# Hybrid attention and gMLP backbone on one core: query projection computed transposed, attention values by column halves of the array, and a new step order ahead of the first output projection

## The chip, the cores and the metric

The program runs on one core of a Trainium2 chip. Five engines with instruction streams of their own work side by side: TensorE (PE in the profile; its weight loads are listed apart as PEld), VectorE (DVE), ScalarE (ACT), GpSimd (POOL) and SyncE (SP), which here only issues transfers. An engine takes its instructions in the order in which they stand. They wait for each other through semaphores. Matmul results land in PSUM (eight banks of 128 partitions by 512 fp32 numbers); everything else stands in SBUF.

The metric is the device time of one execution in microseconds; several runs of one kernel are told by their median. The profile shows one execution. Its span runs from the first to the last instruction of the engines.

## The reference, cut to what matters

A two-layer backbone works on 512 latent tokens and 256 context tokens of width 1024, all in fp32. Layer 0 uses windowed attention with grouped heads; layer 1 uses a gated MLP over chunks. A dense SwiGLU network follows each. Only the latent stream is returned. What the change touches is the attention of layer 0:

```
h_l = modulate(rmsnorm(x, norm_g[0, 0]), sh_ml, sc_ml)          # (512, 1024)
h_c = modulate(rmsnorm(ctx_s, norm_g[0, 0]), sh_mc, sc_mc)      # (256, 1024)
q, k, v = split(h_l @ w_qkv, [1024, 1280])                      # 16 query heads, 4 key/value heads, width 64
q = apply_rope(q, cos, sin) * 64 ** -0.5
k = apply_rope(k, cos, sin)
k_c, v_c = split(h_ctx @ w_qkv[:, 1024:], 2)
# per block of 128 queries: keys of the block before, its own and the next one, and all 256 context keys
p = softmax([q k_band^T + mask, q k_c^T, sink])                 # four query heads share a key/value head
o = p_band v_band + p_ctx v_c
y = o @ w_o
```

`apply_rope` splits a head in two halves of 32 columns: `[x1*c - x2*s, x2*c + x1*s]`.

## The kernel before

**Numbers.** The kernel keeps fp32 accuracy with fp32r matmuls, which are cheaper than fp32 ones: a matrix is split in a high part (rounded to fp32r by ACT, `high`) and a low part (what is left, by DVE or POOL, `low`), and a product is three matmuls, high by high, high by low and low by high (`mm3`). Transposes and the attention values use full fp32; the records show each fp32 matmul as two.

**Stages ahead of the first output projection.** First the token tiles come in (four of x, numbered 0 to 3, two of the context, 4 and 5), are normalised, transposed on PE (`turn_in`) and modulated. The modulation vectors come from eight transfers of 1 MB (`ada0_fetch`) and small matmuls (`ada0_rows`, one 32-column strip of the array each, then `ada0_cols` and `ada0_done`). Then keys and values are projected (`kv`, for eight slices k of the model width and six token tiles), each product streaming 512 columns. Keys are rotated, duplicated along the partitions, transposed (`k_turn`) and split into `khi` and `klo`.

**Queries before.** Query heads come in eight groups p: a key/value head g = p // 2 with its four heads, for one half (256) of the tokens. `q_first` (groups 0 and 1) and `q_step` (the others) project with the tokens as the stationary operand (`q_project`, line 273 to 275): the result has tokens on the partitions and 256 columns. ACT copies it out (`q_rows`), POOL and DVE multiply by the cosine and sine tables (`rotate`), DVE adds (`q_add`), ACT and DVE scale and split into high and low, side by side (`q_split`), PE transposes the four heads for each of two token tiles (`q_turn`, line 759), and ACT copies the transposed tile out (line 760). The partitions of that tile hold 64 high and 64 low parts, and one matmul against the duplicated `khi`, one against `klo`, gives the scores (`score`, line 905).

**Blocks.** Sixteen blocks m (query tile t = m % 4, key/value head g = m // 4) run through `score`, `bound` (mask, row maximum; DVE), `exp` (ACT), `sink`, `total`, `normalise` (POOL), `turn` (PE transposes of the probabilities, line 938), `turned` (copies to SBUF by ACT and DVE), `value` and the store. Blocks at both ends have four key tiles (nb = 4), the others five. `value` (line 958) multiplies a key tile's 128 by 64 values with the probabilities of the four heads, 512 columns; even key tiles use the left 64 columns of the array and odd ones the right, so the two halves of `o_ps` are partial sums over key tiles. ACT copies the right half out (`rows_out`, line 963), and DVE adds both halves into `oT` (`store`, line 969, twice a block).

**Work in between.** The first half of the output projection (`wo_part`, after the first two heads' blocks) and the adaLN rows m2, m4 and m3 (`Ada`: eight multiply-adds on DVE, a fold by a POOL transfer, a mirror by an SP transfer, a stack, and a matmul) run between the blocks. All of this is issued in an order written out by hand, the table `ORDER`: each step's name has a place there, and steps are issued in that order on all engines at once. A step missing in it follows by its planned time.

**Transfers.** SP issues nearly all of them, one after the other; an issue whose buffer is not free, or whose data is not there, holds up those behind it. Weight units (`wfetch`) and adaLN chunks share two buffers of 1 MB (`raw`).

Of the kernel before, what the change touches and what calls it, by code (L numbers as in the profile page):

```python
# [41 lines left out]
x_fetch_4 x_fetch_5 square_in_4 x_fetch_1 warm_0 warm_1 dma dma#2 wfetch_0_0 x_fetch_2 x_fetch_0 x_fetch_3 m2start  # L42
rstd_in_4 square_in_5 square_in_1 warm_2 warm_3 rstd_in_5 rstd_in_1 norm_in_4_0 norm_in_5_1 norm_in_1_0 turn_in_4_0
square_in_2 norm_in_1_1 turn_in_1_0 warm_4 square_in_0 turn_in_5_1 norm_in_5_0 rstd_in_2 norm_in_2_0 turn_in_5_0
ada0_fetch_0 turned_in_4_0 square_in_3 rstd_in_0 turn_in_1_1 turned_in_5_0 turned_in_1_0 turn_in_2_0 ada0_rows_0
rstd_in_3 norm_in_2_1 ada0_rows_out_0 norm_in_3_1 <lambda> norm_in_3_0 ada0_cols_0 turn_in_3_1 turned_in_5_1
ada0_fetch_1 norm_in_0_0 turn_in_0_0 norm_in_0_1 ada0_done_0 turn_in_2_1 ada0_fetch_2 whigh_0_0 wfetch_0_1 ada0_rows_1
modulate0_ctx_0 turn_in_0_1 turn_in_3_0 turned_in_3_1 modulated_ctx_0 ada0_rows_out_1 ada0_fetch_3 turned_in_1_1
wlow_0_0 dma#5 turned_in_2_0 ada0_fetch_4 ada0_cols_1 turned_in_0_0 kv_0_4 turned_in_3_0 ada0_rows_2 modulate0_0
wfetch_1 modulated_high_0 ada0_done_1 turned_in_2_1 ada0_rows_out_2 modulated_low_0 ada0_cols_2 kv_0_2 dma#4 kv_0_3  # L50
modulated_high_1 modulate0_ctx_1 kv_0_5 ada0_done_2 modulate0_1 modulated_ctx_1 whigh_0_1 ada0_fetch_6 ada0_rows_3
norm_in_4_1 turn_in_4_1 ada0_rows_out_3 modulated_low_1 modulate0_ctx_2 kv_1_2 kv_1_4 kv_1_5 turned_in_0_1
turned_in_4_1 modulated_high_2 ada0_cols_3 modulate0_2 modulated_ctx_2 kv_0_0 modulated_low_2 ada0_fetch_5 whigh_1_0
wlow_0_1 ada0_rows_4 wfetch_2 wlow_1_0 whigh_1_1 ada0_done_3 kv_1_3 kv_2_4 ada0_fetch_7 kv_2_5 modulate0_3
ada0_rows_out_4 modulated_high_3 kv_1_0 kv_0_1 kv_2_3 kv_1_1 modulate0_ctx_3 modulated_ctx_3 ada0_cols_4 ada0_done_4
# [148 lines left out]
def backbone_kernel(ctx: ExitStack, tc: tile.TileContext, a, out):  # L204
# [465 lines left out]
    def q_first(p, t, k):  # L670
        if t == 0 and k == 0:
            q_ps[p] = bankA("q0")
        q_project(q_ps[p][:, t * 256:(t + 1) * 256], Q0, 2 * p + t, k)
# [152 lines left out]
    def q_turns(p, i, bank):  # L826
        if i == 0:
            qTs[p] = new_qT()
# [1227 lines left out]
```

## Time and profile before

| What | Value |
|---|---|
| Median of 3 runs | 1110.29 us (1109.47 to 1112.27) |
| Span of the profiled execution | 1108.2 us, granted TensorE clock 0.999 |
| What the median has beside that span | 2.1 us |
| PE busy | 1088.3 us, 98% of the span |
| DVE, ACT, POOL busy | 85%, 55%, 23% of the span |
| First matmul of keys and values | starts at 21.43 us |
| Last matmuls of keys and values | start at 69.22 to 69.69 us |
| First score matmul | starts at 81.08 us |
| First matmul of the output projection proper (`y`, line 281) | starts at 239.24 us |

The profile is of one execution on its one core. In rows of the order of time, a matmul's length is modelled and runs into the next one's; what a matmul costs PE is the distance from its start to the start of the next. Rows of the groups give the mean length of one instruction of a kind and how long its engine had stood idle before it.

### The profile page before, as it was taken

The page shows a single profiled execution, that of the slowest core. Times are in us where ns is not written, and L with a number is a line of the kernel's source. Part 1 is how long each engine was busy: PE and PEld are TensorE (multiplying, and loading weights), DVE is VectorE, ACT ScalarE, POOL GpSimd, SP SyncE. Part 2 cuts the span into 40 slices and gives each one's busy share as a digit, 9 for nine tenths or more (in the row PEclk, how much of TensorE's full clock was granted, in tenths as well). Part 3 has the DMA queues.
Part 4 walks back from the last instruction along what each step waited for, and adds up shares of the span by engine and source line. Part 5 has one row for each costly group of instructions (what it writes and reads, how often), then busy time and mean ns, then how long its engine had stood idle before and what let it go on. Part 6 is the DMA issues. An engine that isn't in the chain of part 4 may idle for free.

```text
span 1108.2 us, 17883 instructions
## 1 busy us (share of the span) xinstructions
PE 1088.3 (98%) x6974; PEld 954.9 (86%) x6974; DVE 943.8 (85%) x1418; ACT 612.6 (55%) x1060; POOL 255.9 (23%) x276
## 2 busy tenths in 40 slices
PE   7999999999999999999999999999999999999997
PEld 4788877768799999998888788887999999998876
DVE  5788988958999999987988778878988888879985
ACT  6457767756555545545665534337555545546652
POOL 2517575624600000001321411006400000002300
PEclk9999999999999999999999999999999999999999
DMA  9652333243245655449964286652233343369821
GB/s 366 266 182 86 136 96 115 77 135 113 109 143 172 224 159 185 171 141 330 225 122 128 68 323 241 205 194 77 70 133 124 132 152 126 126 222 319 158 40 76
DMA packets 48857, 179.15 MB, mean 162 GB/s; under 512 B 4859, under 2 KB 9211, under 8 KB 37637
## 3 DMA queue, kind: packets, MB, share of 16 engines
q1 hardware_dynamic: 41220, 163.34, 42.3%
q0 software_dynamic: 7552, 14.68, 7.9%
q8 instruction: 54, 0.88, 0.3%
q14 instruction: 31, 0.25, 0.1%
HBM read 171.71 MB, written 2.10 MB: 157 GB/s over the span
## 4 chain that ended last, share of the span: by engine, by line
PE 64%; DVE 6%; POOL 2%; issue 2%; ACT 1%; DMA 1%; POOLq 0%; DVEq 0%; SPq 0%; ACTq 0%
PE f L1449 35%; PE y L1633 13%; PE y L1660 4%; PE v L281 4%; PE y L281 2%; PE u L1869 1%; PE u L1867 1%; PE u L1868 1%; POOL tmp L1166 1%; DVE w_lo L224 1%; DVE tmp L1170 1%; DVE x L1154 1%; PE mix L1882 1%; DMA w_raw<-in_w 1%; DVE a_sum L1378 1%
## 5 line engine op out<-in xcount | busy, mean ns | idle before, releaser
L1449 PE MATMUL f<-H,w_hi 128*128 128x256 f32 x960 | 178.6, 284 | 1.1 <-DVE fc L1460 0.5
L1449 PEld LDWEIGHTS f<-H,w_hi 128*128 128x128 f32 x960 | 149.7, 192 | 2.3 <-DVE fc L1460 1.4
L1449 PE MATMUL f<-H,w_lo 128*128 128x256 f32 x480 | 135.8, 283 | 0.0
L1633 PE MATMUL y<-w_hi,s 128*128 128x512 f32 x448 | 120.1, 389 | 0.0
L1449 PE MATMUL f<-S,w_hi 128*128 128x256 f32 x640 | 118.6, 283 | 0.0
L217 ACT CAST w_hi<-w_raw 128x1024 fp32r<-128x1024 f32 x90 | 94.5, 1053 | 39.9 <-PE y L1633 8.9
L217 ACT CAST w_hi<-T 128x1024 fp32r<-128x1024 f32 x80 | 83.7, 1047 | 52.4 <-PE f L1449 33.7
L1456 ACT COPY fc<-f 128x256 f32<-128x256 f32 x120 | 44.6, 372 | 105.8 <-PE f L1449 102.7
L224 DVE TENSOR_TENSOR w_lo<-w_raw,w_hi 128x1024 fp32r<-128x1024 f32 (+1 forms) x81 | 96.3, 1193 | 6.7 <-ACT w_hi L217 6.7
L1449 PEld LDWEIGHTS f<-S,w_hi 128*128 128x128 f32 x640 | 99.9, 192 | 0.0
L1633 PEld LDWEIGHTS y<-w_hi,s 128*128 128x128 f32 x448 | 84.1, 188 | 17.5
L224 DVE TENSOR_TENSOR w_lo<-T,w_hi 128x1024 fp32r<-128x1024 f32 x80 | 97.3, 1216 | 0.0
L1449 PEld LDWEIGHTS f<-H,w_lo 128*128 128x128 f32 x480 | 92.1, 192 | 0.0
L1449 PE MATMUL f<-S,w_lo 128*128 128x256 f32 x320 | 90.7, 284 | 0.5 <-DVE w_lo L224 0.5
L1621 POOL DMA_DIRECT2D t<-in_w x48 | 42.2, 929 | 186.5 <-PE y L1660 88.4
L383 DVE SCALAR_TENSOR_TENSOR acc<-ada_k,sc,acc 128x1024 f32<-128x1024 f32 x56 | 71.6, 1278 | 10.3 <-DMA ada_k<-in_ada 8.4
L397 POOL DMA_DIRECT2D acc<-acc x8 | 6.9, 866 | 314.2 <-DVE acc L383 310.4
L1633 PE MATMUL y<-w_lo,s 128*128 128x512 f32 x224 | 69.1, 390 | 0.6 <-DVE w_lo L224 0.6
L1449 PE MATMUL f<-H,x 128*128 128x256 f32 x480 | 64.3, 283 | 0.0
L932 POOL TENSOR_SCALAR p<-p,st 128x512 f32<-128x512 f32 (+1 forms) x64 | 53.4, 849 | 44.4 <-DVE st L928 11.7
L281 PE MATMUL y<-w_hi,st 128*128 128x512 f32 x224 | 62.3, 391 | 0.0
L1449 PEld LDWEIGHTS f<-S,w_lo 128*128 128x128 f32 x320 | 61.4, 192 | 0.9 <-DVE w_lo L224 0.9
(255 smaller groups left out, 2851.6 us busy)
## 6 DMA issues: line engine op xcount, KB each, us to landing
w_raw<-in_w SPq DMA_DIRECT2D x67, 1024.0 KB, 5.0
ada_k<-in_ada SPq DMA_DIRECT2D x56, 512.0 KB, 5.2
ada_raw<-in_ada SPq DMA_DIRECT2D x12, 1024.0 KB, 4.8
w<-in_w SPq DMA_DIRECT2D x12, 1024.0 KB
t<-in_w POOLq DMA_DIRECT2D x48, 256.0 KB, 6.1
ada<-in_ada SPq DMA_DIRECT2D x8, 1024.0 KB, 11.2
t<-in_w SPq DMA_DIRECT2D x8, 1024.0 KB, 9.2
w_raw<-in_w SPq DMA_DIRECT2D x10, 512.0 KB, 5.6
```

The lines of the kernel that those rows point to most:

```text
L217: nc.scalar.copy(out=hi, in_=src)
L224: (eng or nc.vector).tensor_tensor(out=v(lo), in0=v(src), in1=v(hi).bitcast(F32), op=ALU.subtract)
L281: nc.tensor.matmul(dst, l, w[:, n * 512:(n + 1) * 512], start=first and i == 0, stop=last and i == 2)
L383: nc.vector.scalar_tensor_tensor(out=self.acc, in0=self.raws.pop(k), scalar=sc[:, k:k + 1], in1=self.acc, op0=ALU.mult, op1=ALU.add)
L932: nc.gpsimd.tensor_scalar(out=p, in0=p, scalar1=self.st[:, 12 + j:13 + j], scalar2=1.0, op0=ALU.mult, op1=ALU.mult)
L1154: nc.vector.scalar_tensor_tensor(out=xt, in0=self.tmp[:, c0:c1], scalar=self.r, in1=xt, op0=ALU.mult, op1=ALU.add)
L1166: nc.gpsimd.tensor_tensor(out=self.tmp[:, D:], in0=x[:, self.t, :], in1=self.nxt[0], op=ALU.mult)
L1449: nc.tensor.matmul(dst, l[:, w], r[:, k, :], start=first and k == 0 and j == 0, stop=k == 3 and j == 2, skip_group_check=True)
L1456: nc.scalar.copy(out=self.c[n][:, i * 256:(i + 1) * 256], in_=self.ps[n, 1 if i == 1 else 0])
L1621: nc.gpsimd.dma_start(out=self.tt[:, p * D + 512 * i:p * D + 512 * (i + 1)], in_=a["w"][F2[self.layer] + 1 + 2 * p + i][:, c:c + 512], acc ...
L1633: nc.tensor.matmul(self.bank7(i, j), st[:, c:c + P], w[:, z * 512:(z + 1) * 512], start=i == 1 and p == 0 and l == 0 and z == 0, stop=p == ...
L1660: nc.tensor.matmul(self.y[t][n], st[:, x + t * P:x + (t + 1) * P], parts[h][w][:, n * 512:(n + 1) * 512], start=v == 0 and h == 0 and i == ...
```

## The change

The queries are projected with the weights as the stationary operand. A group p is now two heads (128 columns of the weight) for all 512 tokens, and the result has the heads' 128 columns on the partitions and 512 tokens along the free axis. It needs no transpose. In its place the rotation works across partitions: ACT scales and copies the projection out (`q_rows`), four transfers on SP copy the 32-partition quarters to swapped places (`q_swap`), DVE multiplies by a transposed cosine table (`q_cos`), POOL by a transposed sine table (`q_sin`), DVE adds (`q_add`), and for each head ACT makes the high part (`q_high`) and DVE the low part (`q_low`), which goes to the other 64 partitions. The transposed tables are made once, on PE, by 24 small matmuls against the identity (`rope_turn`, in 32-column strips and in 64-column halves) and two ACT copies (`rope_turned`).

In the values each key tile is multiplied twice, once for the two even heads into the left half of the array and once for the two odd heads into the right half, 256 columns each. The two halves are now two heads' results and not partial sums, and one ACT copy of 128 partitions by 256 columns stores them; `rows_out` and both DVE additions are gone.

The buffers of the probabilities go from 11 to 9, those of the third pair of transposed probabilities from 2 to 1, and `q_X` has 4. The table `ORDER` is written anew. From the first `y` matmul on, every engine's instructions stand in the same order as before (the edit to `sum_a` further down issues the same instructions).

```diff
 ORDER = """
-x_fetch_4 x_fetch_5 square_in_4 x_fetch_1 warm_0 warm_1 dma dma#2 wfetch_0_0 x_fetch_2 x_fetch_0 x_fetch_3 m2start
...
+x_fetch_1 square_in_1 rstd_in_1 norm_in_1_1 x_fetch_5 square_in_5 norm_in_1_0 rstd_in_5 warm_0 warm_1 warm_2 x_fetch_4
...
-    def q_project(dst, u, t, k):
-
-        hi, lo = (p[:, (k % 4) * 256:(k % 4 + 1) * 256] for p in ws.halves[u, k // 4])
-        mm3(dst, HA[:, k, t * P:(t + 1) * P], HA[:, KC + k, t * P:(t + 1) * P], hi, lo, k == 0, k == KC - 1)
...
+    def q_project(p, k):
+
+        c = (k % 4) * 256 + (p % 2) * P
+        hi, lo = (w[:, c:c + P] for w in ws.halves[Q0 + p // 2, k // 4])
+        for i, (w, x) in enumerate(((hi, k), (hi, KC + k), (lo, k))):
+            nc.tensor.matmul(q_ps[p], w, HA[:, x, :], start=k == 0 and i == 0, stop=k == KC - 1 and i == 2)
...
+    def rope_turn(z):
+
+        tables[z] = ps = bankA("rope")
+        n = 32 << z
+        for t in range(NT):
+            for r in range(0, P, n):
+                nc.tensor.matmul(ps[r:r + n, t * P:(t + 1) * P], tables["k"][:, t, 32 * z:32 * z + n], ident,
+                                 start=True, stop=True, tile_position=(0, r))
+
+    def rope_turned(z):
+        nc.scalar.copy(out=ropeT[:, z * SEQ:(z + 1) * SEQ], in_=tables[z])
...
+    def q_rows(p):
+        q_rot[p] = vec("q_rot")
+        nc.scalar.activation(out=q_rot[p][:, 0:SEQ], in_=q_ps[p], func=AF.Copy, scale=HD ** -0.5)
+
+    def q_swap(p):
+
+        for h in range(4):
+            d = 32 * (h ^ 1)
+            dma(q_rot[p][d:d + 32, SEQ:], q_rot[p][32 * h:32 * h + 32, 0:SEQ])
+
+    def q_cos(p):
+        v = q_rot[p][:, 0:SEQ]
+        nc.vector.tensor_tensor(out=v, in0=v, in1=ropeT[:, 0:SEQ], op=ALU.mult)
+
+    def q_sin(p):
+        v = q_rot[p][:, SEQ:]
+        nc.gpsimd.tensor_tensor(out=v, in0=v, in1=ropeT[:, SEQ:], op=ALU.mult)
+
+    def q_add(p):
+        v = q_rot[p][:, 0:SEQ]
+        nc.vector.tensor_tensor(out=v, in0=v, in1=q_rot[p][:, SEQ:], op=ALU.add)
+
+    def q_high(p, z):
+
+        if z == 0:
+            q_X[p] = att_p.tile([P, 2, SEQ], F32R, name="q_X", tag="q_X", bufs=4)
+        r = slice(z * HD, (z + 1) * HD)
+        high(q_X[p][r, z, :], q_rot[p][r, 0:SEQ])
+
+    def q_low(p, z):
+        r, o = slice(z * HD, (z + 1) * HD), slice((1 - z) * HD, (2 - z) * HD)
+        low(q_X[p][o, z, :], q_X[p][r, z, :], q_rot[p][r, 0:SEQ])
...
+            q = q_X[2 * self.g + j // 2][:, j % 2, self.t * P:(self.t + 1) * P]
...
-                    nc.tensor.matmul(dst, self.qT[:, j, :], keys, start=i == 0, stop=i == 1)
+                    nc.tensor.matmul(dst, q, keys, start=i == 0, stop=i == 1)
...
-            self.o = psR_p.tile([P, 512], F32, name="o_ps", tag="o", bufs=1)
+            self.o = psR_p.tile([P, 512], F32, name="o_ps", tag="o", bufs=1)[:, 0:2 * P]
             for i in range(self.nb):
-                v, pt = vals[:, self.kt[i], self.g, :], self.pt[i]
-                if i == self.nb - 1 and i % 2 == 0:
-                    parts = [(z, slice(z * 256, (z + 1) * 256)) for z in range(2)]
-                else:
-                    parts = [(i % 2, slice(0, 512))]
-                for z, c in parts:
-                    nc.tensor.matmul(self.o[z * HD:(z + 1) * HD, c], v, pt[:, c], start=i < 2, stop=i >= self.nb - 2,
+                v, pt = vals[:, self.kt[i], self.g, :], self.pt[i].rearrange("p (c z s) -> p c z s", c=2, z=2)
+                for z in range(2):
+                    nc.tensor.matmul(self.o[z * HD:(z + 1) * HD, :], v, pt[:, :, z, :], start=i == 0, stop=i == self.nb - 1,
                                      tile_position=(0, z * HD), skip_group_check=True)
...
-        def store(self, z):
+        def store(self):
             t, g = self.t, self.g
             dst = oT[g // 2].rearrange("p (c s) -> p c s", c=4)
...
+            nc.scalar.copy(out=dst[:, (g % 2) * 2:(g % 2) * 2 + 2, t * P:(t + 1) * P],
+                           in_=self.o.rearrange("p (c s) -> p c s", c=2))
```

**The order at three places.** The first place is PE at the start of the program, from the first modulation matmuls to the first keys and values (`xT` is a transposed input tile, `rows` and `cols` the modulation, `kv` with `hc` a context tile and with `HA` a latent one). Before:

```order
L526 MATMUL rows<-ada_181,s_90 32x256 x8
L537 MATMUL cols<-ident,rows 128x128 x2
L504 MATMUL xT<-ident,xin 128x128 x12
L526 MATMUL rows<-ada_229,s_90 32x256 x8
L504 MATMUL xT<-ident,xin 128x128 x8
L537 MATMUL cols<-ident,rows 128x128 x2
L273 MATMUL kv<-w_hi,hc 128x512
L274 MATMUL kv<-w_lo,hc 128x512
L275 MATMUL kv<-w_hi,hc 128x512
L526 MATMUL rows<-ada_247,s_90 32x256 x8
```

Now:

```order
L690 MATMUL xT<-ident,xin 128x128 x40
L675 MATMUL rows<-idle 128x256
L712 MATMUL rows<-ada_176,s_90 32x256 x8
L690 MATMUL xT<-ident,xin 128x128 x4
L723 MATMUL cols<-ident,rows 128x128 x2
L690 MATMUL xT<-ident,xin 128x128 x4
L712 MATMUL rows<-ada_214,s_90 32x256 x8
L459 MATMUL kv<-w_hi,hc 128x512
L460 MATMUL kv<-w_lo,hc 128x512
L461 MATMUL kv<-w_hi,hc 128x512
L723 MATMUL cols<-ident,rows 128x128 x2
```

Forty of the 48 transposes now stand ahead of the first modulation matmuls, where 24 stood before, and the first keys and values follow the second modulation product at once.

The second place is PE at the first scores (`s_ps`); `q_ps` is a query projection. Before:

```order
L759 MATMUL qT_ps<-ident,qs 128x128 x4
L273 MATMUL q_ps<-w_hi,HA 128x256
L274 MATMUL q_ps<-w_lo,HA 128x256
L275 MATMUL q_ps<-w_hi,HA 128x256
L273 MATMUL q_ps<-w_hi,HA 128x256
L274 MATMUL q_ps<-w_lo,HA 128x256
L275 MATMUL q_ps<-w_hi,HA 128x256
L273 MATMUL q_ps<-w_hi,HA 128x256
L274 MATMUL q_ps<-w_lo,HA 128x256
L275 MATMUL q_ps<-w_hi,HA 128x256
L905 MATMUL s_ps<-khi,qT 128x512
L905 MATMUL s_ps<-klo,qT 128x512
```

Now:

```order
L856 MATMUL q_ps<-HA,w_hi 128x512 x2
L856 MATMUL q_ps<-HA,w_lo 128x512
L856 MATMUL q_ps<-HA,w_hi 128x512 x2
L856 MATMUL q_ps<-HA,w_lo 128x512
L1095 MATMUL s_ps<-khi,q_X 128x512
L1095 MATMUL s_ps<-klo,q_X 128x512
L1095 MATMUL s_ps<-khi,q_X 128x512
L1095 MATMUL s_ps<-klo,q_X 128x512
L856 MATMUL q_ps<-HA,w_hi 128x512 x2
L856 MATMUL q_ps<-HA,w_lo 128x512
```

The transposes of the queries are gone, and a step of the projection is three matmuls of 512 columns. The whole of group 2 (eight such steps) now stands between the key transposes and the first score, and four steps of group 3 between the second score and the third.

The third place is SP around the start of the blocks (`acc<-acc` is a mirror, `ada_raw` an adaLN chunk, `w_raw` a weight unit, `q_rot` a swap). Before:

```order
L214 DMA w_raw<-in_w 128x2048
L214 DMA acc<-acc 64x1024
L214 DMA ada_raw<-in_ada 128x2048
L214 DMA row<-in_norm_g 128x1024
L214 DMA acc<-in_ada_b 1x1024
L214 DMA w_raw<-in_w 128x2048
L214 DMA acc<-in_ada_b 1x1024
L214 DMA w_raw<-in_w 128x2048
L214 DMA ada_raw<-in_ada 128x2048
```

Now:

```order
L400 DMA w_raw<-in_w 128x2048
L400 DMA q_rot<-q_rot 32x512 x8
L400 DMA w_raw<-in_w 128x2048
L400 DMA row<-in_norm_g 128x1024
L400 DMA acc<-in_ada_b 1x1024
L400 DMA q_rot<-q_rot 32x512 x4
L400 DMA acc<-acc 64x1024
L400 DMA acc<-in_ada_b 1x1024
L400 DMA ada_raw<-in_ada 128x2048
L400 DMA q_rot<-q_rot 32x512 x4
L400 DMA ada_raw<-in_ada 128x2048
L400 DMA w_raw<-in_w 128x2048
```

The swaps of groups 0, 1 and 2 stand ahead of the first mirror, and that of group 3 behind the mirror and an adaLN chunk.

630 lines of the change are left out of this document (382 added, 248 removed).

## The prediction

> **What bounds the kernel now.** I read the page's head first, then busy time by stage, then PE's waits, then PE's rows in order of time. The head:
>
> ```profile
> span 1108.2 us, 17883 instructions
> PE 1088.3 (98%) x6974; PEld 954.9 (86%) x6974; DVE 943.8 (85%) x1418; ACT 612.6 (55%) x1060; POOL 255.9 (23%) x276
> ```
>
> PE is busy nearly always, but its matmuls overlap in the records, so that alone does not say what a stage waits for. Busy time in four stretches (start up to the second modulation product, up to the last keys and values, up to the first output projection matmul, the stage behind it):
>
> ```profile
> 0.00:20.32 20.32, 15.35 (x84) 8.23 (x85) 9.22 (x32) 13.03 (x22) 4.84 (x11) 1.00 0.90 347
> 20.32:70.00 49.68, 49.06 (x319) 37.63 (x316) 39.86 (x77) 20.99 (x35) 15.99 (x20) 1.00 0.72 276
> 70.00:239.24 169.24, 166.47 (x1150) 133.19 (x1148) 145.21 (x312) 121.32 (x264) 97.10 (x121) 1.00 0.35 113
> 239.24:304.00 64.76, 63.72 (x311) 52.60 (x310) 53.25 (x73) 38.91 (x64) 33.60 (x25) 1.00 0.29 99
> ```
>
> The change moves work in the first three. In the second and third PE stands idle for 0.6 and 2.8 us, at full clock; DVE comes next with 145.2 of 169.2 us. The waits of PE in the third stretch:
>
> ```profile
> PE s_ps L905 <- ACT p L916: 1.0, 2, 0.7
> PE o_ps L958 <- DVE oT L969: 0.6, 1, 0.6
> PE qT_ps L759 <- ACT qT L760: 0.3, 1, 0.3
> PE pT_ps L938 <- POOL p L932: 0.3, 1, 0.3
> ```
>
> So from 20 to 239 us the time is PE's own work, and an edit is worth what it takes from PE. Only the start, with 5 us of idle PE in 20, waits for others.
>
> **What a PE instruction costs** is the distance to the next start, not the length shown:
>
> ```profile
> 59.48 0.39 PE L273 MATMUL kv<-w_hi,HA 128*128 128x512 f32 x1
> 60.16 0.28 PE L273 MATMUL q<-w_hi,HA 128*128 128x256 f32 x1
> 60.51 0.40 PE L273 MATMUL kv<-w_hi,HA 128*128 128x512 f32 x1
> ...
> 213.60 1.03 PE L938 MATMUL pT_ps<-ident,p 128*128 128x128 f32 x8
> 214.39 0.48 PE L273 MATMUL q_ps<-w_hi,HA 128*128 128x512 f32 x1
> 214.70 0.39 PE L274 MATMUL q_ps<-w_lo,HA 128*128 128x512 f32 x1
> ```
>
> Three matmuls of 512 columns take 60.16 - 59.48 = 0.68 us, 0.227 each, and three of 256 take 0.35, 0.117 each. The lengths shown (0.39 and 0.28) would make the narrow form look far dearer than it is. Eight transposes take 0.79, and the matmul behind them 0.31 instead of 0.227: (0.79 + 0.08) / 8 = 0.109 each.
>
> **The change part by part, on PE.**
>
> Query transposes, removed:
>
> ```profile
> L759 PE MATMUL qT_ps<-ident,qs 128*128 128x128 f32 x64 | 9.9, 277 | 0.6 <-ACT qT L760 0.3 <-DVE pt L945 0.2
> ```
>
> 64 x 0.109 = 7.0 us less.
>
> Query projection: 8 groups x 2 x 8 x 3 = 384 matmuls of 256 columns become 192 of 512: 384 x 0.117 - 192 x 0.227 = 44.9 - 43.6 = 1.3 us less. The Trainium skill (TensorE: Matmul & The Clock Gate, section "Wait — 56ns, not 53.3ns?") puts the distance at the columns over 2.4 GHz plus about 2.5 ns, 215.7 ns for 512; by that the term would be an estimated 0.5 us. The trace's distances are 0.227 and 0.117, longer than the rule's, and the rows decide.
>
> Rotation tables, added: 24 fp32 matmuls, 48 records of 128 columns, in 32-column strips (32 records) and 64-column halves (16). None stands in the trace; nearest are the modulation matmuls in strips and the values in halves, both 256 or 512 columns:
>
> ```profile
> 31.43 1.07 PE L526 MATMUL rows<-ada,s 128*32 128x256 f32 x16
> 32.43 0.50 PE L273 MATMUL kv<-w_hi,HA 128*128 128x512 f32 x1
> ...
> 209.92 0.60 PE L938 MATMUL pT_ps<-ident,p 128*128 128x128 f32 x4
> 210.45 1.94 PE L958 MATMUL o_ps<-pt,vals 128*64 128x512 f32 x8
> 212.32 0.44 PE L905 MATMUL s_ps<-khi,qT 128*128 128x384 f32 x1
> ...
> 131.15 2.37 PE L958 MATMUL o_ps<-pt,vals 128*64 128x512 f32 x12
> 133.45 0.44 PE L905 MATMUL s_ps<-khi,qT 128*128 128x384 f32 x1
> ```
>
> A strip record of 256 columns costs 1.00 / 16 = 0.0625. With half the columns it is between half of that and all of it: 1.0 to 2.0 us for 32. A half-array record of 256 columns costs 0.1075 (next paragraph): 0.9 to 1.7 us for 16. Together 1.9 to 3.7; I take 2.5, since so short records hardly scale all the way down. A gain is excluded, as nothing is removed for them.
>
> Values: a block with four key tiles takes 212.32 - 210.45 = 1.87 (8 records of 512), one with five 133.45 - 131.15 = 2.30 (8 of 512 and 4 of 256), so the four narrow ones cost 0.43, 0.1075 each, half of a wide one's. The halves therefore work at once already, and pieces of 256 cost nothing extra. Now there are 16 or 20 narrow records for the same columns: 16 x 0.1075 + 0.15 of lead-in = 1.87, and 20 x 0.1075 + 0.15 = 2.30. I take 0. Below, half the lead-in goes: 16 x 0.075 = 1.2 us gain. Above, each record is paced by its weight load:
>
> ```profile
> L958 PEld LDWEIGHTS o_ps<-pt,vals 128*64 128x64 f32 x160 | 10.2, 136 | 17.1 <-issue 14.8 <-ACT st L217 0.8 <-DVE qr L745 0.4
> ```
>
> 16 x 0.136 = 2.18 and 20 x 0.136 = 2.72, that is 0.31 and 0.42 more for 8 blocks each: 5.8 us loss.
>
> The start:
>
> ```profile
> 9.69 0.66 PE L504 MATMUL xT<-ident,xin 128*128 128x128 f32 x4 [1.27 <-DVE xin L481]
> 16.08 1.07 PE L526 MATMUL rows<-ada,s 128*32 128x256 f32 x16
> 19.32 1.07 PE L526 MATMUL rows<-ada,s 128*32 128x256 f32 x16
> 21.43 0.50 PE L273 MATMUL kv<-w_hi,hc 128*128 128x512 f32 x1
> 22.32 1.07 PE L526 MATMUL rows<-ada,s 128*32 128x256 f32 x16
> 24.45 0.50 PE L273 MATMUL kv<-w_hi,HA 128*128 128x512 f32 x1
> 5.16 1.06 ACT L244 ACTIVATE junk<-xin 128x1024 bf16<-128x1024 f32 x1 [1.30 <-DMA xin<-in_ctx]
> 6.52 1.06 ACT L244 ACTIVATE junk<-xin 128x1024 bf16<-128x1024 f32 x1 [0.21 <-DMA xin<-in_ctx]
> ```
>
> The three modulation products go by their transfers, and as many bytes stand ahead of the first as before, so they stay near 16.1, 19.3 and 22.3. Behind the second, transposes held the keys and values until 21.43; now these may start at 20.3, have a second context tile (0.68) done ahead of the third product, and go on with latent tiles behind it at 23.3 instead of 24.45. With the last four transposes done too that is up to 2.2 us. Against it, the identity now comes behind five token tiles instead of three. Tiles land 6.52 - 5.16 = 1.36 apart, so the first transpose moves from 9.69 towards 11 to 12, and forty of them (4.4 us) must end by 16: about nothing to spare, and what is late there is late one for one. I take 1.5 less, bounds 2.2 less and 1 more.
>
> **Beside PE.** DVE loses the two additions of each block and its query work stays at 32 instructions of this size; ACT and POOL shift little:
>
> ```profile
> L969 DVE TENSOR_TENSOR oT<-o_ps,o_sb 64x256 f32<-64x256 f32 x32 | 13.3, 416 | 1.7 <-ACT o_sb L963 1.2
> L731 POOL TENSOR_TENSOR qr<-qsb,rope x16: 726/738/923, 72.2 to 196.9; 128x256 f32<-128x256 f32 x16
> L745 DVE TENSOR_TENSOR qr<-qr x8: 673/684/1006, 75.6 to 200.6; 128x512 f32<-128x512 f32 x8
> L751 ACT ACTIVATE qs<-qr x8: 618/626/653, 76.3 to 201.5; 128x512 fp32r<-128x512 f32 x8
> 77.26 0.52 SPq L214 DMA_DIRECT2D acc<-acc  x1
> acc<-acc SPq DMA_DIRECT2D x8, 256.0 KB, 2.9
> SPq L214 <- DMA acc<-acc: 14.8, 1, 14.8
> ```
>
> About 13 us leave DVE: nothing in the sum, as PE waited for DVE 0.6 us. The new chain of a group is copy 0.6, four issues on SP at 0.52 and a landing like a mirror's 2.9 (5.0 together), sine on POOL 2 x 0.74, addition 0.7, high 0.6, low 0.7: 9.1 us. The tightest is group 1, whose last projection stands ahead of the key transposes (24 x 0.109 = 2.6), group 2's steps (24 x 0.227 = 5.4), two scores (0.9) and four steps of group 3 (2.7): 11.6 us of PE work cover it. I cost it at nothing; without that cover it costs what is missing. PE's small waits at the first scores for the exponentials stay, as two score banks still take turns. I leave the 2.8 us of idle time, with 2 less to 4 more as bounds.
>
> **Sum against the span:** -7.0 - 1.3 + 2.5 + 0 - 1.5 + 0 = -7.3 us, 1108.2 to 1100.9. Behind 239 us the order is the same, so the stage starts earlier and keeps its length. The median of the runs shown is 1110.29, 2.1 above the span: 1110.29 - 7.3 = 1103.
>
> **Rivals.**
>
> More than the sum: DVE's 13 us free the waits at the scores and stores (1.4 us), the start gives its full 2.2 and the values 1.2. 0.7 + 1.2 + 1.4 more: 1099.7. For it speaks DVE at 86% of the third stretch, against it that PE hardly waited for DVE.
>
> Values paced by weight loads: 5.8 back, 1108.8. Against it speaks the 0.1075 of four narrow records in a row, for it that sixteen to twenty in a row stand nowhere. The Trainium skill (TensorEngine Tiling (Array Packing), section "Restrictions and Gotchas") says that column tiling excludes the fast weight load, which speaks against twice as many loads in halves; in the trace a half's load takes 0.136 and does not show in the distances.
>
> The gain ends at the border: in the next stage PE shares the path with DVE, ACT and POOL (63.7 and 53.3 of 64.8 us), and m3's fold, mirror and stack could keep their time while PE comes early. All of the 7.3 may go: 1110.
>
> SP's order makes it slower: group 3's swap stands behind the mirror, for which SP once waited 14.8 us. 14.8 + 9.1 = 24 us against, by the prices above, 30 us of PE work from group 3's last step to its first score. It decides beyond a wait of 21 us; then group 3, the next weight unit and the swaps behind are late together, and with 32 us the kernel is 11 - 7.3 = 4 us slower: 1114.
>
> **How the numbers follow.** Forecast 0.58, more 0.17, weight loads 0.09, border 0.08, SP 0.08. No change means within 0.3%, 3.3 us, about what a measurement of this kernel can tell: 1107.0 to 1113.6. Faster gets the forecast's bulk (0.54), all of more (0.17), and a third of the two cases near the bound (0.06): 0.77. Slower gets SP's, 0.07 with a rest below it; the same 0.16. The forecast's own range is 1099 to 1107; with the other cases 1097 to 1109.
>
> **What would show it.** Right: the query projection as 192 matmuls at 0.227, no query transposes, values at 1.87 and 2.30, the first `y` matmul near 232 (239.24 - 7.3), and from there the same length. Wrong: values at 2.2 and 2.7; a wait of PE for `q_X` or of SP for the mirror over 20 us; keys and values that start later than 21.4; a first `y` at 232 with the span near 1108.

## The result, and the profile after

| | before | changed |
|---|---|---|
| time, median of 4 runs each, side by side | 1109.88 us (1108.33 to 1112.27) | 1103.5 us (1102.31 to 1104.95) |
| ratio, 95% interval | | 0.9945 (0.993 to 0.9959) |
| span of the profiled execution | 1108.2 us | 1101.8 us |
| first output projection matmul `y` | 239.24 us | 234.53 us |

The kernel is 0.55% faster, within half a microsecond of the forecast of 1103; against the kernel before, run beside it, the gain is 6.4 us, where 7.3 was forecast. It got there by other steps than the forecast: the start gained twice as much as forecast, and about 5 us of what the transposes gave was lost again to a new wait. The page's head of the changed kernel:

```profile
span 1101.8 us, 17762 instructions
PE 1081.2 (98%) x6894; PEld 949.5 (86%) x6894; DVE 945.6 (86%) x1386; ACT 606.7 (55%) x1054; POOL 255.3 (23%) x268
```

Its busy time in the first three stretches, the second and third of which end with the same events as before to within 0.2 us, while the first ends ahead of the second modulation product and not behind it (start, end, length, then PE, weight loads, DVE, ACT and POOL with their instructions, the granted clock, DMA share and GB/s):

```profile
0.00:19.10 19.10, 14.74 (x80) 9.06 (x80) 11.01 (x33) 13.23 (x22) 3.87 (x10) 1.00 0.90 343
19.10:68.68 49.58, 49.58 (x345) 37.33 (x344) 38.90 (x73) 20.89 (x36) 16.24 (x21) 1.00 0.76 287
68.68:234.53 165.85, 160.07 (x1046) 126.77 (x1044) 146.79 (x284) 116.34 (x259) 101.39 (x117) 0.99 0.42 130
```

Three things stand in these rows. The keys and values end 1.1 us earlier (their last matmul starts at 68.55, before at 69.69), although the table matmuls now stand ahead of their end. The third stretch is only 3.4 us shorter (169.24 to 165.85; from that last matmul to the first `y` it is 3.6), although PE does 6.4 us less in it (166.47 to 160.07): PE's idle time rose from 2.8 to 5.8 us, and the clock fell below 1.00. And DVE does not do less there, but 1.6 us more (145.21 to 146.79). PE's waits in that stretch, in us in total, times and the longest:

```profile
PE pT_ps L1128 <- DVE pt L1135: 2.5, 1, 2.5
PE s_ps L1095 <- ACT p L1106: 1.1, 1, 1.1
PE q_ps L856 <- DVE klo L410: 1.1, 1, 1.1
PE ada_ps L596 <- DVE pt L1135: 0.8, 1, 0.8
```

The first of them is the one to follow. PE's rows in order of time around it (start and length in us, what PE waited for in brackets):

```profile
140.85 0.39 PE L856 MATMUL q_ps<-HA,w_lo 128*128 128x512 f32 x1
143.70 0.63 PE L1128 MATMUL pT_ps<-ident,p 128*128 128x128 f32 x4 [2.46 <-DVE pt L1135]
145.45 0.39 PE L1095 MATMUL s_ps<-khi,q_X 128*128 128x256 f32 x1 [1.11 <-ACT p L1106]
```

DVE's rows at the same place:

```profile
138.12 4.72 DVE L410 TENSOR_TENSOR q_X<-q_rot,q_X 64x512 fp32r<-64x512 f32 x1
142.87 0.69 DVE L1135 COPY pt<-pT_ps 128x512 f32<-128x512 f32 x1
```

And POOL's:

```profile
137.84 0.84 POOL L583 DMA_DIRECT2D acc<-acc  x1
138.49 2.58 POOL L1122 TENSOR_SCALAR p<-p,st 128x640 f32<-128x640 f32 x3
140.81 1.48 POOL L950 TENSOR_TENSOR q_rot<-q_rot,ropeT 128x512 f32<-128x512 f32 x1
```

The busy time in two slices there, columns as above:

```profile
140.00:145.00 5.00, 1.87 (x11) 1.19 (x9) 4.97 (x6) 0.49 (x1) 2.28 (x3) 1.00 0.16 30
145.00:150.00 5.00, 4.55 (x21) 3.88 (x23) 3.32 (x10) 4.34 (x12) 2.16 (x3) 0.66 0.31 75
```

A low split of the new query chain (`q_low`, group 4) takes 4.72 us on DVE, where the same instruction takes 0.69 elsewhere. It ends at 142.84, which is 0.55 after POOL's run of instructions ends (140.81 + 1.48 = 142.29). The copy of turned probabilities queued behind it is what PE waits for, the exponentials behind that copy come late too, and for the next 5 us the granted clock is 0.66. The Trainium skill (SBUF — State Buffer, section "SBUF: two separate sides") says that a DVE instruction with two inputs in SBUF and a POOL instruction that reads SBUF lock each other out of a shared port for the length of an instruction; these rows agree, but here the lock lasted over four POOL instructions in a row. Those four overlap in the records (138.49 + 2.58 = 141.07, and the last one starts at 140.81); the last section comes back to this.

DVE's groups in the score stage show that this is the largest case of many. The query work of the kernel before (busy us, mean ns of one, idle time ahead of it):

```profile
L732 DVE TENSOR_TENSOR qr<-qsb,rope 128x256 f32<-128x256 f32 x16 | 7.7, 521 | 0.0
L752 DVE SCALAR_TENSOR_TENSOR qs<-qr,qs 128x512 fp32r<-128x512 f32 x8 | 6.3, 786 | 0.2 <-ACT qs L751 0.2
L745 DVE TENSOR_TENSOR qr<-qr 128x512 f32<-128x512 f32 x8 | 6.0, 751 | 0.0
```

That of the changed kernel:

```profile
L410 DVE TENSOR_TENSOR q_X<-q_rot,q_X 64x512 fp32r<-64x512 f32 x16 | 17.4, 1095 | 0.5
L946 DVE TENSOR_TENSOR q_rot<-q_rot,ropeT 128x512 f32<-128x512 f32 x8 | 8.3, 1039 | 0.0
L954 DVE TENSOR_TENSOR q_rot<-q_rot 128x512 f32<-128x512 f32 x8 | 5.4, 681 | 0.1
```

Before, 20.0 us; now 31.1 us, of which 32 x 0.69 = 22.1 is work and 9 us is standing still. With the block additions (12.9 us in that stretch) the sum before was 32.9, so DVE was relieved by less than 2 us, not by 13.

The other terms, in PE's rows: the two table steps, the two forms of the values, and the end of the query projection ahead of the key transposes.

```profile
42.98 1.09 PE L910 MATMUL rope<-ident,rope 128*64 128x128 f32 x16
44.01 1.07 PE L712 MATMUL rows<-ada,s 128*32 128x256 f32 x16
44.89 1.06 PE L910 MATMUL rope<-ident,rope 128*32 128x128 f32 x32
45.88 0.50 PE L459 MATMUL kv<-w_hi,HA 128*128 128x512 f32 x1
...
229.32 2.38 PE L1144 MATMUL o_ps<-pt,vals 128*64 128x256 f32 x20
231.63 1.09 PE L1128 MATMUL pT_ps<-ident,p 128*128 128x128 f32 x8
232.66 1.95 PE L1144 MATMUL o_ps<-pt,vals 128*64 128x256 f32 x16
234.53 0.73 PE L467 MATMUL y<-w_hi,st 128*128 128x512 f32 x2
...
73.53 0.61 PE L856 MATMUL q<-HA,w_hi 128*128 128x512 f32 x2
73.99 0.39 PE L856 MATMUL q<-HA,w_lo 128*128 128x512 f32 x1
74.22 2.78 PE L1015 MATMUL kT<-ident,kr 128*128 128x128 f32 x24
```

The tables cost 1.03 + 0.99 = 2.0 us, the values 2.31 and 1.87, and three projection matmuls 74.22 - 73.53 = 0.69, 0.23 each.

### The profile page after: what moved, and what is told of

The parts are those of the page before. It is cut to its first block, busy times and chain, and to the rows that moved or that the text cites. A ratio compares the mean times of both kernels' runs of the same rounds, so it can differ in the third digit from the quotient of the medians.

```text
span 1101.8 us, 17762 instructions
## 1 busy us (share of the span) xinstructions
PE 1081.2 (98%) x6894; PEld 949.5 (86%) x6894; DVE 945.6 (86%) x1386; ACT 606.7 (55%) x1054; POOL 255.3 (23%) x268
## 4 chain that ended last, share of the span: by engine, by line
PE 83%; DVE 7%; DMA 3%; issue 2%; POOL 2%; ACT 2%; SPq 1%; DVEq 0%; POOLq 0%; ACTq 0%
PE f L1618 35%; PE y L1802 13%; PE y L467 5%; PE y L1829 4%; PE v L467 4%; PE s_ps L1095 2%; PE q_ps L856 2%; PE o_ps L1144 2%; PE pT_ps L1128 2%; PE u L2036 1%; PE u L2038 1%; PE u L2037 1%; POOL tmp L1335 1%; PE kv L459 1%; PE kv L461 1%
## 5 line engine op out<-in xcount | busy, mean ns | idle before, releaser
L410 DVE TENSOR_TENSOR w_lo<-w_raw,w_hi 128x1024 fp32r<-128x1024 f32 (+1 forms) x81 | 95.8, 1189 | 7.0 <-ACT w_hi L403 5.0
L410 DVE TENSOR_TENSOR w_lo<-T,w_hi 128x1024 fp32r<-128x1024 f32 x80 | 97.2, 1215 | 0.0
L1106 ACT ACTIVATE p<-s_ps,st 128x512 f32<-128x512 f32 (+1 forms) x64 | 47.5, 742 | 28.7 <-DVE st L1101 22.5
```

The source lines that it names most:

```text
L410: (eng or nc.vector).tensor_tensor(out=v(lo), in0=v(src), in1=v(hi).bitcast(F32), op=ALU.subtract)
L1106: nc.scalar.activation(out=p[:, 0:self.n], in_=self.s[j], func=AF.Exp, scale=-1.0, bias=self.st[:, 4 + j:5 + j], accum_out=self.st[:, 8 + ...
```

## The experiments

Ratios are against the kernel before, run beside each of them; a difference between two kernels is that of their ratios times 1110 us. Two ratios with intervals of about 0.0015 to each side leave such a difference uncertain by about 2 us.

| run | median us | ratio (95%) | against |
|---|---|---|---|
| e1 changed kernel again | 1104.8 | 0.9951 (0.9938 to 0.9965) | |
| e2 late low split | 1099.52 | 0.9907 (0.9892 to 0.9922) | e1: -4.9 |
| e3 64 transposes more | 1109.07 | 0.9989 (0.9977 to 1.0001) | e1: +4.2 |
| e4 projection in 256 columns | 1107.04 | 0.9968 (0.9957 to 0.998) | e1: +1.9 |
| e5 late split, 64 transposes more | 1106.67 | 0.9973 (0.9962 to 0.9983) | e2: +7.3 |
| e6 late split, table from the host | 1106.51 | 0.9961 (0.9947 to 0.9974) | e2: +6.0 |
| e7 late split, old start | 1111.97 | 1.0018 (1.0009 to 1.0027) | e2: +12.3 |
| e8 late split, additions back on DVE | 1113.06 | 1.0025 (1.0014 to 1.0036) | e2: +13.1 |
| e9 one sine product on DVE | 1101.04 | 0.9919 (0.9902 to 0.9936) | e1: -3.6 |
| e10 late split, all sine products on DVE | 1101.18 | 0.9918 (0.9903 to 0.9933) | e2: +1.2 |
| e11 late split, key transposes split | 1101.87 | 0.9918 (0.9902 to 0.9935) | e2: +1.2 |
| e12 kernel before, new start alone | 1110.58 | 1.0003 (0.9994 to 1.0012) | before: +0.3 |

**The new wait: e1, e2 and e9.** The changed kernel again, without an edit:

> The changed kernel once more, as the base of the runs beside it. Expected 1103.5 us again. What matters is the low split of group 4 on DVE, which took 4.72 us instead of 0.69 and held PE for 2.5 us at 141 and 1.1 us at 144. If the cause is the order of instructions on DVE and POOL, it stands in this profile at the same place with the same length; if it was an accident of one execution, the place shows 0.7 us and PE does not wait there.

Its low split took 4.72 us at 138.31, PE waited 3.0 and 0.9 us, and the time was 1104.8: it is no accident of one execution. Behind these waits its clock was 0.50 from 145 to 150 us.

In e2 one name moves in the order; e9 moves one instruction to another engine:

```diff
 e2
-... q_step_6_4 normalise_5_1 q_low_4_0 m4fold ... turned_4_2 turned_4_3 exp_6_2 ...
+... q_step_6_4 normalise_5_1 m4fold ... turned_4_2 turned_4_3 q_low_4_0 exp_6_2 ...
 e9
-... q_step_7_0 q_sin_5 sink_6 q_add_5 ...
+... q_step_7_0 sink_6 q_sin_5 q_add_5 ...
-        nc.gpsimd.tensor_tensor(out=v, in0=v, in1=ropeT[:, SEQ:], op=ALU.mult)
+        (nc.vector if p == 5 else nc.gpsimd).tensor_tensor(out=v, in0=v, in1=ropeT[:, SEQ:], op=ALU.mult)
```

> The low split of group 4's first half moves behind the two probability copies that DVE makes for block 4, so that no PE instruction waits for what stands behind it. Theory (DVE stood still because POOL ran four instructions in a row, and the copies queued behind it were what PE waited for): PE's waits of 2.5 and 1.1 us go, and with them the granted clock of 0.66 that follows them, about 1 us: 3 to 5 us less than the changed kernel, 1098.5 to 1100.5. Rival (the third stretch is held by DVE's whole load, and a wait removed here comes back at the next copy): within 1 us of the changed kernel.

> The changed kernel, with one instruction moved: the sine product of group 5 runs on DVE, just ahead of the addition that needs it, and not on POOL behind three normalisations. DVE's order up to the long low split is untouched. Theory (an addition of DVE with two operands in SBUF stands still until POOL's run of instructions ends, and then takes its 0.55 us): POOL's run now ends 1.2 us sooner, with its third normalisation, and the low split takes 3.5 us instead of 4.72; PE's wait behind it falls from about 2.5 to 1.3 us, and the kernel is 1 to 2.5 us faster than the changed one, 1101 to 1102.5. Rival (the split waits for something else, such as the weight and modulation transfers of 130 to 138 us): it keeps 4.7 us.

The rows of POOL and DVE in order of time, of e2; in this kernel and the next the lines are numbered 7 higher, so that L417 is L410 of the changed kernel:

```profile
140.95 1.49 POOL L957 TENSOR_TENSOR q_rot<-q_rot,ropeT 128x512 f32<-128x512 f32 x1
140.52 2.48 DVE L417 TENSOR_TENSOR q_X<-q_rot,q_X 64x512 fp32r<-64x512 f32 x1
```

The same of e9:

```profile
138.89 2.58 POOL L1129 TENSOR_SCALAR p<-p,st 128x640 f32<-128x640 f32 x3
138.52 3.49 DVE L417 TENSOR_TENSOR q_X<-q_rot,q_X 64x512 fp32r<-64x512 f32 x1
```

In e9 POOL's run ends at 141.47 and the split at 142.01, 0.54 later: 3.49 us, where 3.5 was expected. In e2 the split stands elsewhere and again ends 0.56 after POOL's run (142.44, 143.00), but nothing that PE needs is queued behind it. So the length is set by POOL's run, and the loss by what stands behind the split. The time agrees for e2 (3 to 5 us expected, 4.9 measured), though not all that was expected to go did: PE still waits 1.21 us for the exponentials at 144.94. What is gone is the first wait and the slow clock (1.00 from 140 to 155 us). For e9 the median, 1101.04, is at the lower end of the 1101 to 1102.5 expected, but against e1 the 3.6 us are more than the 1 to 2.5 us: PE waited 1.7 us in place of 3.0, and in e9 the clock held 1.00 behind it, where e1 had 0.50. e2 is the fastest kernel of the study.

**The transposes: e3 and e5.** Each block turns its first key tile twice, in e3 in the changed kernel, in e5 in e2:

```diff
-            for j in range(GRP):
-                nc.tensor.transpose(ps[:, j * P:(j + 1) * P], ...)
+            for _ in range(2 if i == 0 else 1):
+                for j in range(GRP):
+                    nc.tensor.transpose(ps[:, j * P:(j + 1) * P], ...)
```

> Every block turns its first key tile twice into the same bank: 64 transposes of 128 columns more on PE, as many as the change took away, with no new wait. Theory (PE's own work sets the time): 64 x 0.109 = 7.0 us more than the changed kernel, 1110.5. Rival (PE stood idle 5.8 us of this stretch, so DVE's chain sets its end and the transposes taken away gained little): 1.5 to 4 us more.

> The kernel with the late low split, and 64 transposes more on PE as in the run with repeated turns. There 4.3 us were lost, not 7.0. Theory (PE's own work sets the time, and the missing 2.7 us came out of the wait at 141 us, which hid part of them): with that wait gone nothing hides them, 1099.5 + 7.0 = 1106.5. Rival (transposes are cheaper to the span than their distance on PE, because other engines set part of the stretch): 1099.5 + 4.3 = 1103.8.

With the new wait in place 64 transposes cost 4.2 us, just above the rival's range and short of the 7.0 of the theory; without it they cost 7.3 (7.0 expected). The executions of e3 spread from 1105.3 to 1111.87 us, and its profile is of a fast one (1106.36, clock 1.00 behind the wait). In it PE's first wait shrank from 3.0 to 1.8 us and that for `ada_ps` (0.8) was gone: PE's extra work filled time in which it stood idle. So PE's own work does set the time, and 7 us is the right price of the transposes, except where the change itself made PE wait.

**The width of the projection: e4.**

```diff
-            nc.tensor.matmul(q_ps[p], w, HA[:, x, :], start=k == 0 and i == 0, stop=k == KC - 1 and i == 2)
+            for c2 in (0, 256):
+                nc.tensor.matmul(q_ps[p][:, c2:c2 + 256], w, HA[:, x, c2:c2 + 256], start=..., stop=...)
```

> The query projection with 384 matmuls of 256 columns in place of 192 of 512, everything else as changed. By the distances of the rows (0.117 and 0.227): 192 x (0.234 - 0.227) = 1.3 us more than the changed kernel. Rival (weight loads of 0.19 us behind each narrow matmul become the pace, since two narrow ones share one weight but load it twice): 192 x 2 x (0.19 - 0.117) = 28 us more. By the Trainium skill (TensorE: Matmul & The Clock Gate, section "Wait — 56ns, not 53.3ns?"), whose rule adds 2.5 ns to each matmul, it would be an estimated 0.5 us.

This kernel opens the sums of both column halves in one bank, and its queries are not those of the reference; its instructions are as described. PE's rows:

```profile
71.00 0.64 PE L857 MATMUL q<-HA,w_hi 128*128 128x256 f32 x4
71.48 0.40 PE L857 MATMUL q<-HA,w_lo 128*128 128x256 f32 x2
71.72 0.64 PE L857 MATMUL q<-HA,w_hi 128*128 128x256 f32 x4
```

Six narrow matmuls take 0.72, 0.120 each, so the form costs 192 x (0.240 - 0.227) = 2.5 us; 1.9 was measured, with an uncertainty of 2. The term was of the right kind and small, and 28 us for a pace by weight loads is excluded. The time alone cannot tell the expected 1.3 from the 0.5 of the skill's rule; the rows, with 2.5, are nearer to the 1.3.

**DVE as the cover: e8 and e10.**

```diff
+            for z in range(2):
+                junk = att_p.tile([HD, 2 * P], F32, name="junk", tag="junk", bufs=1)
+                nc.vector.tensor_tensor(out=junk..., in0=self.o[0:HD, :]..., in1=kept[0:HD], op=ALU.add)
```

> The kernel with the late low split, and each block makes two additions of 64x256 on DVE again, from the product bank and the copied half into a tile that nobody reads: 32 x 0.416 = 13.3 us of DVE, as in the kernel before, and the bank comes free 0.8 us later. Theory as predicted (DVE's load costs nothing, PE hardly waits for it): within 1 us, 1099 to 1100.5. Rival (DVE is the second bound of this stretch, at 147 of 166 us, and stands in the chain of PE's waits): 3 to 8 us more.

The rival is right by more than its range: 13.3 us of DVE cost 13.1 us. The busy time of e8 from its last keys and values to its first `y`:

```profile
69.36:245.17 175.81, 162.40 (x1046) 126.32 (x1045) 157.43 (x315) 117.09 (x259) 101.78 (x117) 1.00 0.39 123
```

PE's waits in it from 85 us on, the first, the second and a later one:

```profile
PE s_ps L1102 <- ACT p L1113: 3.2, 4, 1.3
PE pT_ps L1135 <- DVE pt L1142: 2.6, 4, 1.3
...
PE o_ps L1151 <- DVE junk L1161: 1.0, 2, 0.5
```

In the kernel before the first of these waits came to 1.0 us. In e8 PE stands idle for 175.81 - 162.40 = 13.4 us of the stretch, where it was 4.1 in e2, spread over many small waits behind DVE; that is 9.3 of the 12.6 us by which the stretch is longer than e2's, and the rest stands in PE's modelled lengths. Part of it is the later release of the product bank, 1.0 us by the last row. So DVE, with 146 of 163 us busy in e2, has no room left for 13 us in this order of steps: without the additions taken away, the new query chain would have been paid for on the span. e8 does not tell DVE's load from the place of the additions: each of them also stands ahead of copies that PE needs. In e10 the eight sine products move to DVE:

```diff
-        nc.gpsimd.tensor_tensor(out=v, in0=v, in1=ropeT[:, SEQ:], op=ALU.mult)
+        nc.vector.tensor_tensor(out=v, in0=v, in1=ropeT[:, SEQ:], op=ALU.mult)
```

> The kernel with the late low split, and all eight sine products on DVE, each just ahead of its addition: DVE gets 8 x 0.69 = 5.5 us more work, and POOL loses the eight instructions of 1.3 to 1.5 us during which DVE's cosine products stood still (1.1 us each in three groups). Theory (DVE's load sets the pace of the score stage, and one us of DVE is about one us of the span, as with the additions put back): 5.5 us of work less 3 to 4 us of standing still, 1 to 2.5 us slower, 1100.5 to 1102. Rival (only the standing still counts, since DVE still has gaps): 1 to 3 us faster.

DVE's busy time stays (145.84 us in that stretch, against 145.99 in e2): the 6.1 us of sine products on it are made up by instructions that stand still less. The time is 1.2 us more than e2's, within what the theory expected, but within the uncertainty of no change too.

**The tables: e6.** The table is made on the host and comes in one transfer; the matmuls and the two copies are gone.

```diff
         dma(tables["k"], a["rope"])
+        dma(ropeT, a["ropeT"])
-    at(W + 27, rope_turn, 0)
-    at(W + 27.5, rope_turned, 0)
-    at(W + 28, rope_turn, 1)
-    at(W + 28.5, rope_turned, 1)
```

> The kernel with the late low split, and the turned rotation table comes from the host as one 512 KB transfer: the 48 table matmuls on PE and the two copies on ACT are gone. Theory: the matmuls' distance in the profile, 1.0 us for the 32 strips and about as much for the 16 halves, comes back: 2.0 us less, 1097.5. Rival (the transfer, at 45 us, where the queues are busy 0.76 of the time, makes a modulation or weight transfer late): no gain or up to 2 us more.

It is 6.0 us slower. A row of ACT in e6:

```profile
45.27 1.04 ACT L410 CAST w_hi<-w_raw 128x1024 fp32r<-128x1024 f32 x1 [1.44 <-DMA w_raw<-in_w]
```

A row of PE behind it:

```profile
46.65 0.44 PE L730 MATMUL cols<-ident,rows 128*128 128x128 f32 x2 [1.95 <-ACT rows L724]
```

And the busy time of the slice that follows:

```profile
47.00:51.00 4.00, 4.00 (x12) 3.16 (x12) 1.38 (x3) 1.80 (x3) 2.88 (x5) 0.58 0.57 231
```

The rival is right, and its price was too low. The weight transfer behind the table lands late, ACT's cast waits 1.4 us for it, the copy of modulation rows queued behind the cast keeps PE idle for 1.95 us, and the next 4 us run at a clock of 0.58. The key transposes then start at 75.75, 1.9 us later than in e2 (73.87). Of the other 3.4 us up to the first `y` (236.67 against 231.41), 2.4 are idle time of PE in the score stage (6.5 us against 4.1); where these waits come from was not followed up.

**The start: e7 and e12.** e7 puts the steps up to the third modulation product into the old order, in e2; e12 puts the new order, up to `kv_0_1`, into the kernel before.

```diff
 e7
-x_fetch_1 square_in_1 rstd_in_1 norm_in_1_1 x_fetch_5 ... turn_in_4_0 wfetch_0_0 turned_in_4_0 turn_in_4_1 ...
+x_fetch_4 x_fetch_5 square_in_4 x_fetch_1 warm_0 warm_1 dma dma#2 wfetch_0_0 ... kv_0_4 ada0_rows_2 kv_0_5 ...
 e12
-x_fetch_4 x_fetch_5 square_in_4 x_fetch_1 warm_0 ... kv_0_4 turned_in_3_0 ada0_rows_2 ... kv_0_3 ...
+x_fetch_1 square_in_1 rstd_in_1 norm_in_1_1 x_fetch_5 ... kv_0_4 ada0_cols_1 kv_0_5 ... ada0_rows_2 ... kv_0_1 m2start ...
```

> The kernel with the late low split, and the steps up to the third modulation product in the order of the kernel before (the two context products of the first modulation chunk keep their places around the third product; two more transposes come late). Theory (the start's gain reaches the end one for one, as PE has no idle time between 20 us and the scores): the first keys and values were 1.15 us earlier in the changed kernel, and a second context product and four transposes stood ahead of the first latent one, so 1.2 to 2.5 us more, 1100.7 to 1102. Rival (the third product waits for its transfer in both, so the order ahead of it is free): within 0.5 us.

> The kernel before, with one part of the change alone: its steps up to the last latent product of the first modulation chunk stand in the new order, all steps behind them in their old order. Theory (the start gained about 3 us, not 1.5: the last product of keys and values came 1.1 us earlier in the changed kernel although 2.0 us of table matmuls stood ahead of it): 3 us less than the kernel before. As forecast: 1.5 us less. Rival (the gain needs the new order of the later steps as well, or the kernel before gives it back where its key transposes and first scores wait): within 1 us of the kernel before.

PE's rows of e7 in order of time, where the keys are turned:

```profile
77.23 2.78 PE L1022 MATMUL kT<-ident,kr 128*128 128x128 f32 x24
87.33 1.19 PE L863 MATMUL q_ps<-HA,w_hi 128*128 128x512 f32 x2 [7.31 <-DVE klo L417]
```

PE's rows of e12, the first latent product and the wait behind it:

```profile
22.99 0.50 PE L273 MATMUL kv<-w_hi,HA 128*128 128x512 f32 x1
...
29.64 0.50 PE L275 MATMUL kv<-w_hi,HA 128*128 128x512 f32 x1 [1.72 <-DVE HA L224]
```

Both theories missed; e12 came out as its rival said. In e7 the old start itself costs 77.23 - 73.87 = 3.4 us at the key transposes; the rest of its 12.3 us is another matter: the first projection step of the score stage waits 7.31 us, until the last key split (DVE, up to 87.18) has read its bank, where it waited 1.1 us for an early one in e2, and up to 90 us the clock behind that wait is 0.50. That it inherits another PSUM bank with the other order of the start is likely but not shown. In e12 the first latent keys and values come as early as in the changed kernel (22.99; before 24.45), and a new wait of 1.72 us takes it back, followed by a clock of 0.60 in the slice from 30 to 33 us: the last keys and values start at 70.80, 1.1 us later than before. That profile is of the slowest of twelve executions (1113.64 us); the median shows no gain either. So the start's gain is neither free nor a thing by itself: it needs the later steps in their new order.

**The bank: e11.** An attempt at the wait of 1.1 us for `klo`:

```diff
-q_first_1_4 q_first_1_5 q_first_1_6 q_first_1_7 ... k_turn_0 ... q_rows_1 ... k_split_0_0 k_split_0_1 ...
+q_first_1_4 q_first_1_5 k_turn_0 q_first_1_6 q_first_1_7 ... k_split_0_0 k_split_0_1 q_rows_1 ...
```

> The kernel with the late low split; the first eight key transposes go ahead of the last two steps of group 1's projection, and the first two key splits ahead of the copy of group 1's rows, so that the bank that the first projection step of the score stage waits for is read out sooner. Theory (PE waits 1.1 us there for the low part of the second split): that wait goes, and 0.5 to 1.1 us of the span with it, 1098.4 to 1099. Rival (the wait is for another bank, or the rows of group 1 and its rotation come later and make the first scores of block 4 late): no gain, or 1 to 7 us more.

The rival is right: the wait shrinks to 0.4 us, but the rows of group 1 come later, and the second score waits 0.99 us for its low part and the next projection 0.39 us for a copy; behind these two the clock is 0.57 from 86 to 90 us. It is 1.2 us slower than e2, within the uncertainty.

## Why the prediction was right, and where it was not

The sum again, each step as forecast and as the two profiles and the runs show it (us of span):

| step | forecast | measured | from |
|---|---|---|---|
| query transposes | -7.0 | -7.3 | e5 |
| projection of 512 columns | -1.3 | -1.9 | e4 |
| rotation tables | +2.5 | +2.0 | rows at 42.98 and 44.89 |
| values | 0 | 0 | 2.31 and 1.87 |
| start | -1.5 | -3.0 | last matmul of keys and values: -1.1 in all, without +2.0 tables and -0.2 projection |
| idle time and clock of the third stretch | 0 | +4.6 | -3.6 in all from there to the first `y`, without -7.0 and -1.1 projection |
| stage behind | 0 | -1.7 | 867.3 after the first `y`, before 869.0 |

With the forecast's own -7.0 and -1.3 the measured rest gives -7.0 - 1.3 + 2.0 + 0 - 3.0 + 4.6 - 1.7 = -6.4, the difference of the two spans. The figures of e4 and e5 are uncertain by about 2 us. The two rows of rests come from one execution of each kernel: with the same steps up to there, the first latent product starts anywhere between 22.46 (e3) and 23.95 us (e8), so a single profile tells the term of the start to about 1 us.

**Right.** What bounds the kernel (PE's own work), the price of a transpose, the price of the narrow values (0.1075 a record, so that weight loads in halves did not show), and the tables within their bounds. None of the three rivals for a smaller gain came about: SP's wait for the mirror in the third stretch was 7.6 us, and the stage behind did not grow. No wait of PE for `q_X` stands in the third stretch, so the chain of 9.1 us was covered.

**Wrong in size: the start.** The term was argued from the first products alone, where the gain is 24.45 - 23.10 = 1.35 us plus the second context product and the four last transposes done ahead of them, 0.68 + 0.44: 2.5 in all, beyond the 2.2 allowed. The forecast took 1.5 because the transposes might end late; they started at 10.59, not at 11 to 12, and forty of them were done by 15.12. The order of the later steps kept the gain and added to it; e12 shows that without them it is lost.

**Wrong in kind: "About 13 us leave DVE: nothing in the sum".** Both halves of that sentence failed. DVE was not relieved, since the 32 new instructions have two inputs in SBUF and stood still for 9 us while POOL worked (the old ones for about 3); the durations were taken from rows in which that hardly shows. And what DVE has to do does count: in e8 13.3 us of it cost 13.1. The idle term had its bound at +4; it was 4.6, of which 3.0 is idle time of PE and about 1.7 (5 us at 0.66) the clock behind the gap. The forecast asked whether a score would wait for the query chain, and priced the chain's length against PE's cover. It did not ask what is queued on DVE behind an instruction of that chain: a copy that PE needs at once. e2 takes 4.9 us back by asking that.

The total came out right because the start's extra 1.5 us, the tables' 0.5 and the 1.7 us of the stage behind (whose length varied from 866.4 to 869.6 us over the runs of all these kernels, so that this may be no effect at all) made up most of the 4.6. That is luck: of the prediction's own signs of being right, the first `y` near 232 did not come (234.53). With the low split moved, in e2, it stands at 231.41.

## What to carry to other kernels

When a change moves work to an engine that waits for nobody, list what stands behind each new instruction on that engine, and ask what happens if it takes as long as its neighbour's run of work; a move in the order of one such instruction was worth 5 us here, as much as most of the change. An engine at 88% of a stretch is not cover: price the next 13 us on it as if it were the bound, unless a run shows otherwise. A gain at the start counts only with an order behind it that can use it.

## What the runs showed of the hardware

- **DVE stands still for the POOL instruction that it meets, and for a whole run where POOL's instructions overlap.** The low split of 0.69 us took 4.72 (4.72 again in e1), 3.49 in e9 and 2.48 in e2, each time up to 0.54 to 0.56 us after POOL's run. DVE copies out of PSUM took 0.69 beside the same run (e2, at 139.80). Elsewhere DVE gets in between two POOL instructions, as these rows of the changed kernel show, of DVE and then of POOL:

```profile
78.57 0.69 DVE L410 TENSOR_TENSOR q_X<-q_rot,q_X 64x512 fp32r<-64x512 f32 x1
120.83 1.15 DVE L410 TENSOR_TENSOR q_X<-q_rot,q_X 64x512 fp32r<-64x512 f32 x1
119.99 1.44 POOL L410 TENSOR_TENSOR w_lo<-w_raw,w_hi 128x256 fp32r<-128x256 f32 x2
121.41 1.80 POOL L1122 TENSOR_SCALAR p<-p,st 128x512 f32<-128x512 f32 x2
```

The first split met no POOL instruction. The second ends 0.55 us after the POOL instruction that it met (the second of `w_lo`, up to 121.43), although POOL had two more ready. In the twelve traces with the new query chain, all 128 DVE instructions of the chain that took over 0.76 us between 85 and 240 us end 0.53 to 0.56 us after the end of a POOL instruction. It is the one that they met at their start (or the next, where they started within 0.06 us of a border) and they take at most 1.8 us, except at the one place of the long split. Only there do POOL's records overlap in these traces, by 0.19 to 0.27 us; elsewhere between 85 and 240 us, and in the kernel before, it is 0.06 at most. The overlap begins with POOL's DMA issue at 137.84, which has normalisations ready right behind it. Whether that issue causes it, no run tests; the rows of the kernel before could not have told the length.
- **A short gap costs more than its length.** Behind 1.95 us of idle PE the clock was 0.58 for 4 us (e6), behind 1.72 us it was 0.60 (e12), behind 2.46 and 1.11 us 0.66 over 5 us (changed kernel), behind 2.97 and 0.91 us 0.50 over 5 us (e1), behind 0.99 and 0.39 us 0.57 over 4 us (e11); behind 1.85 us (e3) and behind 1.71 and 1.12 us (e9) it stayed 1.00. The Trainium skill (TensorE: Matmul & The Clock Gate, section "What's actually happening") gives the clock back to idle after an idle window of about 3.4 us; here gaps of half that length and less were sometimes enough, and sometimes not.
- **Narrow matmuls on one weight.** Two of 256 columns cost 0.240 against 0.227 for one of 512 (e4), in full stream.
